# Strassen's scheme on pairs of feed-forward units, and the output projection in three blocks

## The chip, the cores and the metric

The kernel runs on one core of one Trainium2 chip. Its time is device microseconds from launch to end, the median of the runs. TensorE (PE) multiplies, VectorE (DVE), ScalarE (ACT) and GpSimd (POOL) do the elementwise work, and SyncE (SP) issues most of the DMAs.

## The reference

Two layers of an encoder trunk on 512 tokens of width 1024, in float32. Each layer has a feed-forward part, a token mixer with three branches, cross-attention into 256 memory tokens, and a second feed-forward part. The change touches the feed-forward parts alone:

```python
def rms_norm(x, g):
    xf = x.astype(jnp.float32)
    y = xf * lax.rsqrt(jnp.mean(xf * xf, axis=-1, keepdims=True) + EPS)
    return (y * g.astype(jnp.float32)).astype(x.dtype)

def swiglu(h, w_in, w_out):
    a, b = jnp.split(h @ w_in, 2, axis=-1)
    return (jax.nn.silu(a) * b) @ w_out
...
    for l in range(DEPTH):
        x = x + 0.5 * swiglu(rms_norm(x, ffn1_norm[l]), ffn1_w_in[l], ffn1_w_out[l])
...
        x = x + 0.5 * swiglu(rms_norm(x, ffn2_norm[l]), ffn2_w_in[l], ffn2_w_out[l])
```

`D_FF` is 2816, so `w_in` is 1024 x 5632 (a half for `a`, a half for `b`) and `w_out` is 2816 x 1024.

## The kernel before

Activations are held transposed: width on the 128 partitions (`KD` = 8 tiles, index k or m), the 512 tokens along the free dimension. Every matrix product keeps float32 accuracy by splitting both operands into a high part (type fp32r) and a low part, the rest. `mm3` issues three matmuls for a product: high x high, high x low, low x high.

Weights come from HBM as a stream in an order that `plan` fixes. `Stream.load` issues a DMA of a chunk (at most 128 x 2048) on SP's queue into one of `NSTAGE` = 2 staging tiles. `Stream.split` makes the high part on ACT (`whi`, L346) and the low part on DVE (`wlo`, L347) for up to 1024 columns, a "part"; there are `NW` = 4 buffers for each. `Stream.take` hands a part to the caller and first splits up to `LOOK` = 3 parts ahead.

A feed-forward call goes over 22 units of 128 columns of each half of `w_in` in 2 blocks of 11. In a unit, `pair_unit` fills two PSUM banks (psa, psb) with 2 x 8 x 3 matmuls of 512 columns, on x times the gain without the norm's row factor (`xh`, `xl`). The factor `s_row` is applied on the way out: DVE multiplies psa by it (L552), ACT takes the Silu (L553), POOL multiplies by it again (L554), DVE multiplies by psb (L555), and `split_to` makes the high and low parts (ACT L494, DVE L495). After a block, for each of 8 m, a bank takes 11 x 3 matmuls of the output projection and DVE adds half of it to x (L582). After the last block of a call, `nxt.tile(m)` writes the next norm's `xh`, `xl` (L428, L429) and sums squares (ACT L437, POOL L438). In the last call of the program the last m is done in two halves of 256 tokens, so that the final norm can begin with the first half.

Side tasks (generators in `tasks`) are advanced by `tick`. `mem_stats` is one: it loads the memory tokens and a table of constants and computes the norm of the memory. It is queued at the start of the program. `lam_prep` and others are held back with `issue_after`; otherwise a scheduler orders each engine's queue, and that order isn't always the order of the program. The engines run their queues in order. Buffers of the arena (`get`, `getr`) are quarters, halves or wholes of 14 tiles of 128 x 2048.

The mixer's rotary embedding runs on POOL (L747, L752, L754) beside DVE's work. The projection of the cross-attention keys (`xk`) uses `pair_unit` on the 256 memory tokens, so its matmuls have 256 columns.

Of the kernel before, what the change touches and what calls it, by code (L numbers as in the profile page):

```python
# [14 lines left out]
P = 128  # L15
# [10 lines left out]
NB = 2  # L26
JB = NJ // NB
# [46 lines left out]
def plan():  # L74
# [12 lines left out]

    def ffn(l, w_in, w_out):
        for b in range(NB):
            for j in range(b * JB, (b + 1) * JB):  # L90
                first = l == 0 and j == 0 and w_in == "ffn1_w_in"
                add((w_in, l, j), [256, 256, 512, 1024] if first else [1024, 1024], block(w_in, l, 0, KD, (j * P, D_FF + j * P), P))
            for m in range(KD):
                add((w_out, l, b, m), [768, 640], block(w_out, l, b * JB, JB, (m * P,), P))

# [168 lines left out]
def emit(tc, wts, par, rows, ws_t, bd, xt, memt, const, out):  # L264
# [40 lines left out]
    class Stream:  # L305
        def __init__(self):
            self.parts = []
            off = 0
            self.off = []
            for i, (key, cols, _) in enumerate(chunks):  # L310
                self.off.append(off)
                c0 = 0
                for n in cols:
                    self.parts.append((i, c0, n))
                    c0 += n
                off += c0 * P
# [4 lines left out]
            self.pos = 0  # L321

        def load(self, parts=None, between=None, eng=sp):
# [4 lines left out]
            t = stage_p.tile([P, 2048], F32, tag="stage", name="stage")  # L328
# [9 lines left out]

        def split(self):
            i, c0, n = self.parts[self.n_split]  # L340
            while i and self.n_load <= i + NSTAGE - 1 and self.n_load < len(chunks):
                self.load()
            t = self.loaded[i][:, c0:c0 + n]
# [6 lines left out]
            if c0 + n == sum(chunks[i][1]):  # L350
                del self.loaded[i]

        def take(self, key):
            i, c0, n = self.parts[self.pos]
            assert chunks[i][0] == key, (chunks[i][0], key)
# [178 lines left out]
    def ffn(l, w_in, w_out, norm, nxt):  # L534
        row, held = [], []
# [3 lines left out]

        for b in range(NB):  # L540
            gs = []
            for j in range(b * JB, (b + 1) * JB):
                held.append(pair_unit(w_in, l, j, xhk, xlk, hook=finish if norm is first and j == 1 else None))
                if norm is first and j == 0:
                    continue
                if not row:
                    finish()
                s_row = row[0]
                for psa, psb in held:
                    t = get(1)  # L550
                    g = getr(2)
                    dve.tensor_tensor(t.f, psa, s_row, op=ALU.mult)  # L552
                    mark["silu"] = act.activation(t.f, t.f, AF.Silu).ins  # L553
                    pool.tensor_tensor(t.f, t.f, s_row, op=ALU.mult)  # L554
                    dve.tensor_tensor(t.f, t.f, psb, op=ALU.mult)  # L555
                    mark["lo"] = split_to(g.r[:, 0:512], g.r[:, 512:1024], t.f)
                    t.free()
                    gs.append(g)
                    tick()
                held = []  # L560
            for m in range(KD):
                if b == NB - 1 and m == KD - 1 and isinstance(nxt, FinalNorm):
                    parts = [ws.take((w_out, l, b, m)) for _ in range(2)]
                    for h in range(2):
                        cs = slice(h * 256, h * 256 + 256)
                        ps = bank()[:, 0:256]
                        for k in range(JB):
                            hi, lo = parts[k // 6]
                            c = slice(k % 6 * P, (k % 6 + 1) * P)
                            mm3(ps, hi[:, c], lo[:, c], gs[k].r[:, 0:512][:, cs], gs[k].r[:, 512:1024][:, cs],  # L570
                                k == 0, k == JB - 1)
                        dve.scalar_tensor_tensor(x[:, m, cs], ps, 0.5, x[:, m, cs], op0=ALU.mult, op1=ALU.add)
                        nxt.half(h)
                    continue
                ps = bank()
                for h, (k0, k1) in enumerate(((0, 6), (6, 11))):
                    hi, lo = ws.take((w_out, l, b, m))
                    for k in range(k0, k1):
                        c = slice((k - k0) * P, (k - k0 + 1) * P)
                        mm3(ps, hi[:, c], lo[:, c], gs[k].r[:, 0:512], gs[k].r[:, 512:1024],  # L580
                            k == 0, k == JB - 1)
                dve.scalar_tensor_tensor(x[:, m], ps, 0.5, x[:, m], op0=ALU.mult, op1=ALU.add)  # L582
                if b == NB - 1:
                    nxt.tile(m)
                tick()
            for g in gs:
                g.free()
# [751 lines left out]
    tasks.append(mem_stats())  # L1339
# [30 lines left out]
```

## Time and profile before

| | before |
|---|---|
| median of 3 runs | 2640.4 us (2640.38 to 2642.13) |
| the profiled execution | 2639.9 us |
| its span in the profile | 2638.1 us |
| mean granted clock of TensorE | 0.998 of full |
| PE, DVE, ACT, POOL busy | 99%, 52%, 44%, 15% |
| matmuls in the trace | 12213 |
| HBM read | 250.27 MB, 96 GB/s over the span |

The profile describes one execution; its span runs from the first to the last instruction, and the time holds 1.8 us around it. Busy shares are averages over the whole span. Matmuls are pipelined: the duration that a row gives is longer than the distance to the next start, so rates are read from starts.

### The profile page before, as it was taken

What the parts mean: (1) busy time and instruction counts of PE and PEld (TensorE: products, weight loads), DVE (VectorE), ACT (ScalarE), POOL (GpSimd) and SP (SyncE); (2) the same over time, 40 slices, a digit from 0 to 9 for tenths busy, and PEclk for the clock granted to TensorE, in tenths of its full rate; (3) what the DMA queues carried; (4) which work ended last, traced back from release to release, by engine and by line L of the source; (5) the groups of instructions that cost most, each with busy time, mean ns of one, the idle gap of its engine ahead of it and who ended that gap; (6) DMA issues with size and microseconds to landing.
All of it is one profiled execution on the core that took longest, in us unless ns stands there. A gap on an engine that the chain in (4) does not pass through costs nothing.

```text
span 2638.1 us, 30190 instructions
## 1 busy us (share of the span) xinstructions
PE 2619.2 (99%) x12213; PEld 2183.8 (83%) x12213; DVE 1373.7 (52%) x1972; ACT 1164.3 (44%) x1659; POOL 390.5 (15%) x294
## 2 busy tenths in 40 slices
PE   9999999999999999999999999999999999999998
PEld 7888888788888888888888888887888888888886
DVE  5434457766656554334443344577675655543443
ACT  5322337967635442222332223479575444432223
POOL 1101115100021021011111011151000300210111
PEclk9999999999999999999999999999999999999999
DMA  5232232122233222232222322321222231322222
GB/s 182 81 133 96 82 108 83 67 90 72 96 108 116 88 104 91 93 112 81 103 96 87 127 96 78 119 87 56 88 80 104 96 128 64 112 86 99 111 76 76
DMA packets 49979, 254.31 MB, mean 96 GB/s; under 512 B 5168, under 2 KB 10928, under 8 KB 31664
## 3 DMA queue, kind: packets, MB, share of 16 engines
q1 hardware_dynamic: 49120, 250.30, 26.8%
q10 hardware_dynamic: 720, 2.09, 0.2%
q8 instruction: 95, 1.56, 0.2%
q14 instruction: 44, 0.36, 0.0%
HBM read 250.27 MB, written 2.10 MB: 96 GB/s over the span
## 4 chain that ended last, share of the span: by engine, by line
PE 95%; ACT 3%; DVE 1%; DMA 0%; issue 0%; DVEq 0%; ACTq 0%; POOL 0%; POOLq 0%
PE ps L367 30%; PE ps L365 30%; PE ps L366 30%; PE ps L891 1%; PE ps L879 1%; PE ps L862 1%; ACT whi L346 0%; DMA x<-in_xt 0%; PE ps L1192 0%; DVE slot L495 0%; ACT L668 0%; ACT L678 0%; ACT slot L1002 0%; PE ps L403 0%; DVE slot L481 0%
## 5 line engine op out<-in xcount | busy, mean ns | idle before, releaser
L346 ACT CAST whi<-stage 128x1024 fp32r<-128x1024 f32 (+2 forms) x506 | 491.4, 973 | 1002.5 <-PE ps L366 873.8
L347 DVE TENSOR_TENSOR wlo<-stage,whi 128x1024 fp32r<-128x1024 f32 (+2 forms) x506 | 587.3, 1162 | 471.9 <-ACT whi L346 470.0
L365 PE MATMUL ps<-xh,whi 128*128 128x512 f32 x2048 | 801.4, 391 | 5.0 <-DVE slot L1015 3.3
L366 PE MATMUL ps<-xl,whi 128*128 128x512 f32 x2048 | 798.0, 390 | 0.3 <-DVE xl L429 0.3
L367 PE MATMUL ps<-xh,wlo 128*128 128x512 f32 x2048 | 797.8, 390 | 0.0
L365 PE MATMUL ps<-slot,whi 128*128 128x512 f32 (+1 forms) x1291 | 487.5, 378 | 0.0
L366 PE MATMUL ps<-slot,whi 128*128 128x512 f32 (+1 forms) x1291 | 486.5, 377 | 0.0
L367 PE MATMUL ps<-slot,wlo 128*128 128x512 f32 (+1 forms) x1291 | 486.4, 377 | 0.0
L365 PEld LDWEIGHTS ps<-xh,whi 128*128 128x128 f32 x2048 | 384.8, 188 | 86.6 <-DVE slot L1015 4.9
L366 PEld LDWEIGHTS ps<-xl,whi 128*128 128x128 f32 x2048 | 385.0, 188 | 80.1 <-DVE xl L429 0.9
L367 PEld LDWEIGHTS ps<-xh,wlo 128*128 128x128 f32 x2048 | 384.8, 188 | 80.0
L554 POOL TENSOR_TENSOR slot<-slot,srow 128x512 f32<-128x512 f32 x88 | 148.2, 1685 | 921.2 <-ACT slot L553 921.2
L366 PEld LDWEIGHTS ps<-slot,whi 128*128 128x128 f32 x1291 | 243.0, 188 | 45.0 <-issue 0.5
L365 PEld LDWEIGHTS ps<-slot,whi 128*128 128x128 f32 x1291 | 242.9, 188 | 44.8 <-issue 0.5
L367 PEld LDWEIGHTS ps<-slot,wlo 128*128 128x128 f32 x1291 | 242.9, 188 | 44.6
L494 ACT CAST slot<-slot 128x512 fp32r<-128x512 f32 (+2 forms) x149 | 89.4, 608 | 296.6 <-DVE slot L555 216.3
L552 DVE TENSOR_TENSOR slot<-ps,srow 128x512 f32<-128x512 f32 x88 | 60.7, 691 | 214.1 <-PE ps L367 214.0
L438 POOL TENSOR_TENSOR nacc<-nacc,slot 128x512 f32<-128x512 f32 x55 | 84.4, 1535 | 550.0 <-ACT slot L437 284.1
L495 DVE TENSOR_TENSOR slot<-slot,slot 128x512 fp32r<-128x512 f32 (+2 forms) x149 | 105.5, 717 | 90.5 <-ACT slot L494 90.4
L555 DVE TENSOR_TENSOR slot<-slot,ps 128x512 f32<-128x512 f32 x88 | 60.5, 688 | 107.4 <-POOL slot L554 107.4
L495 DVE TENSOR_TENSOR slot<-ps,slot 128x512 fp32r<-128x512 f32 (+1 forms) x144 | 92.8, 655 | 39.5 <-ACT slot L494 38.7
L494 ACT CAST slot<-ps 128x512 fp32r<-128x512 f32 (+1 forms) x144 | 77.3, 562 | 56.4 <-PE ps L367 54.2
(194 smaller groups left out, 2252.2 us busy)
## 6 DMA issues: line engine op xcount, KB each, us to landing
stage<-in_wts SPq DMA_DIRECT2D x140, 1024.0 KB, 4.8
stage<-in_wts SPq DMA_DIRECT2D x64, 704.0 KB, 4.0
stage<-in_wts SPq DMA_DIRECT2D x77, 512.0 KB, 3.2
stage<-in_wts SPq DMA_DIRECT2D x8, 768.0 KB, 4.3
slot<-in_memt SPq DMA_DIRECT2D x6, 512.0 KB, 3.7
slot<-in_bd SPq DMA_DIRECT2D x4, 512.0 KB, 6.0
out<-slot SPq DMA_DIRECT2D x8, 256.0 KB, 2.5
x<-in_xt SPq DMA_DIRECT2D x1, 1024.0 KB, 8.4
```

Source lines behind the costliest of these rows:

```text
L346: mark["whi"] = act.copy(hi[:, 0:n], t).ins
L347: dve.tensor_tensor(lo[:, 0:n], t, hi[:, 0:n].bitcast(F32), op=ALU.subtract)
L365: pe.matmul(ps, lhsT=ah, rhs=bh, start=start, stop=False)
L366: pe.matmul(ps, lhsT=ah, rhs=bl, start=False, stop=False)
L367: pe.matmul(ps, lhsT=al, rhs=bh, start=False, stop=stop)
L438: self.adder.tensor_tensor(self.acc, self.acc, sq.f, op=ALU.add)
L494: act.copy(hi, src)
L495: return dve.tensor_tensor(lo, src, hi.bitcast(F32), op=ALU.subtract).ins
L552: dve.tensor_tensor(t.f, psa, s_row, op=ALU.mult)
L554: pool.tensor_tensor(t.f, t.f, s_row, op=ALU.mult)
L555: dve.tensor_tensor(t.f, t.f, psb, op=ALU.mult)
L862: pe.matmul(ps, lhsT=qt[e].r[:, c0:c0 + P], rhs=kk.r[:, k0:k0 + 512], start=part == 0, stop=part == 1)
```

## The change

Of the 22 units of a call, 4 stay as they were. The other 18 are done as 9 pairs. For a pair the weights of two units are seen as a 2 x 2 matrix of quarters (units by halves of k), for `a` and for `b`, and the activations as 2 x 2 quarters (halves of k by halves of the tokens). A scheme in Strassen's (Winograd's) form computes the same four output quarters from 7 products of sums of quarters instead of 8. In the code one product has both units of output side by side in one PSUM bank: 2 x 4 x 3 matmuls of 256 columns. The sums on the weights' side (S1 to S4) are made by POOL in `Stream.source` from the staged chunks P and Q, before the split; those on the activations' side by `combos` and `in_place`, once for a call, on x times gain times row factor. Seven products are combined by DVE on their way out of PSUM (`add`).

The blocks are `FB` = ((4, 2), (0, 4), (0, 3)): 4 units and 2 pairs, then 4 pairs, then 3 pairs, so the output projection runs in 3 blocks of 8, 8 and 6 k-steps. Its weight parts are one of 1024 or 768 columns for each m instead of two of 768 and 640. Pairs alternate between the staging tiles and two arena tiles (`slots`). `mem_stats` is queued before the last block's output projection in the first call.

```diff
-NB = 2
-JB = NJ // NB
+FB = ((4, 2), (0, 4), (0, 3))
...
+            for i in range(npair):
+                a, g = (j * P, j * P + P), (D_FF + j * P, D_FF + j * P + P)
+                side = (npair - i) % 2
+                add((w_in, l, "P", j, side), [2048], blocks(w_in, l, [(0, c) for c in a + g]))
+                add((w_in, l, "Q", j, side), [2048], blocks(w_in, l, [(4, c) for c in g + a]))
+                j += 2
             for m in range(KD):
-                add((w_out, l, b, m), [768, 640], block(w_out, l, b * JB, JB, (m * P,), P))
+                add((w_out, l, b, m), [(j - j0) * P], block(w_out, l, j0, j - j0, (m * P,), P))
...
+        PAIR = ("A11", "S1", "S2", "A12", "S3", "S4", "A22")
...
+        def room(self, i):
+            n = sum(self.side(j) == self.side(i) for j in self.loaded)
+            return n < (2 if self.side(i) and self.slots else 0 if self.side(i) else NSTAGE)
...
+        def source(self, i, nm):
+
+            a11, a21 = self.loaded[i][:, 0:1024], self.loaded[i][:, 1024:2048]
+            a22, a12 = self.loaded[i + 1][:, 0:1024], self.loaded[i + 1][:, 1024:2048]
+            if nm == "A11":
+                self.sums = [get(2), get(2)]
+                s1, s2 = (r.f for r in self.sums)
+                pool.tensor_tensor(s1, a21, a22, op=ALU.add)
+                pool.tensor_tensor(s2, s1, a11, op=ALU.add)
+                pool.tensor_tensor(a21, a21, a11, op=ALU.add)
+            s1, s2 = (r.f for r in self.sums)
+            if nm == "S4":
+                pool.tensor_tensor(s2, s2, a12, op=ALU.add)
+            return {"A11": a11, "S1": s1, "S2": s2, "A12": a12, "S3": a21, "S4": s2, "A22": a22}[nm]
...
-            while i and self.n_load <= i + NSTAGE - 1 and self.n_load < len(chunks):
+            while i and self.n_load <= i + pair + 3 and self.n_load < len(chunks) and self.room(self.n_load):
                 self.load()
...
+        def combos():
+            xn.extend([get(4), get(4)])
+            for m in range(KD):
+                dve.scalar_tensor_tensor(xn[m // 4].f[:, m % 4 * 512:(m % 4 + 1) * 512], x[:, m],
+                                         norm.gain[:, m:m + 1], row[0], op0=ALU.mult, op1=ALU.mult)
+            yield
+            b11, b12, b21, b22 = (quarter_of(h, t) for h in range(2) for t in range(2))
+            f = {}
+            for nm, a, b, op in (("S1", b11, b12, ALU.subtract), ("S2", b22, "S1", ALU.add),
+                                 ("S3", b12, b22, ALU.subtract), ("A22", b21, "S2", ALU.subtract)):
+                r = get(2)
+                c = r.f.rearrange("p (k c) -> p k c", k=4)
+                pool.tensor_tensor(c, a, f[b][1] if isinstance(b, str) else b, op=op)
+                f[nm] = r, c
+            for nm in ("S1", "S2", "S3", "A22"):
+                o = getr(4)
+                split_to(o.r[:, 0:1024], o.r[:, 1024:2048], f[nm][0].f)
...
+        def in_place():
+            for nm, h, t in (("A11", 0, 0), ("A12", 1, 0), ("S4", 1, 1)):
+                hi, lo = (a[:, 4 * h:4 * h + 4, t * 256:(t + 1) * 256] for a in (xh, xl))
+                split_to(hi, lo, quarter_of(h, t))
...
+            def product(nm):
+                ps = bank()
+                hi, lo = ws.take((w_in, l, "P", j), nm)
+                mh, ml, _ = mv[nm]
+                for i in range(2):
+                    for k in range(4):
+                        c = slice(i * 512 + k * P, i * 512 + (k + 1) * P)
+                        mm3(ps[:, i * 256:(i + 1) * 256], hi[:, c], lo[:, c], mh[k], ml[k],
+                            i == 0 and k == 0, i == 1 and k == 3)
+                return ps
...
+            act.copy(q1.f, product("A11"))
+            p5 = product("S1")
+            add(two(u2.f), product("S2"), q1, ALU.subtract)
+            add(two(w.f), p5, u2, ALU.subtract)
+            add(a4[:, :, 0], product("A12"), q1)
+            act.activation(a4[:, :, 0], a4[:, :, 0], AF.Silu)
+            p7 = product("S3")
+            add(two(u3.f), p7, u2)
+            add(b4[:, :, 1], p7, w, ALU.subtract)
+            add(a4[:, :, 1], product("S4"), w)
+            mark["silu"] = act.activation(a4[:, :, 1], a4[:, :, 1], AF.Silu).ins
+            add(b4[:, :, 0], product("A22"), u3)
...
+            dve.tensor_tensor(av.f, av.f, bv.f, op=ALU.mult)
+            g = getr(4)
+            mark["lo"] = split_to(g.r[:, 0:1024], g.r[:, 1024:2048], av.f)
...
+        for b, (nc, npair) in enumerate(FB):
+            for _ in range(nc):
                 held.append(pair_unit(w_in, l, j, xhk, xlk, hook=finish if norm is first and j == 1 else None))
...
+                if ws.slots is None:
+                    ws.slots = [get(4), get(4)]
+                    tasks.append(combos())
+                for ps in held:
+                    gated(*ps)
                     tick()
                 held = []
+            if nc:
+                drain()
+                in_place()
+            for _ in range(npair):
+                pair(j)
+                j += 2
+                tick()
...
+                if norm is first:
+                    tasks.append(mem_stats())
...
+                tail = last and m == KD - 1 and isinstance(nxt, FinalNorm)
+                for h in range(2 if tail else 1):
+                    cs = slice(h * 256, h * 256 + 256) if tail else slice(0, 512)
+                    ps = bank()[:, 0:cs.stop - cs.start]
+                    for k in range(nj):
+                        c = slice(k * P, (k + 1) * P)
+                        mm3(ps, hi[:, c], lo[:, c], gs[k][0][:, cs], gs[k][1][:, cs], k == 0, k == nj - 1)
+                    dve.scalar_tensor_tensor(x[:, m, cs], ps, 0.5, x[:, m, cs], op0=ALU.mult, op1=ALU.add)
...
-    tasks.append(mem_stats())
```

`gated` holds the six instructions that followed a unit before, unchanged.

## Rows read from the trace of the kernel before

**Rows 1.** The page, part 1: busy us, share of the span, instructions of each engine.

```profile
PE 2619.2 (99%) x12213; PEld 2183.8 (83%) x12213; DVE 1373.7 (52%) x1972; ACT 1164.3 (44%) x1659; POOL 390.5 (15%) x294
```

**Rows 2.** The page, part 4: the chain that ended last, shares by engine and line.

```profile
PE 95%; ACT 3%; DVE 1%; DMA 0%; issue 0%; DVEq 0%; ACTq 0%; POOL 0%; POOLq 0%
...
PE ps L367 30%; PE ps L365 30%; PE ps L366 30%; PE ps L891 1%; PE ps L879 1%; PE ps L862 1%; ACT whi L346 0%; DMA x<-in_xt 0%; PE ps L1192 0%; DVE slot L495 0%; ACT L668 0%; ACT L678 0%; ACT slot L1002 0%; PE ps L403 0%; DVE slot L481 0%
```

**Rows 3.** PE's waits: engine, line, releaser: us in total, times, longest.

```profile
PE ps L365 <- DVE slot L1015: 3.3, 2, 1.6
```

**Rows 4.** Timeline of PE in a feed-forward unit: start us, duration us, line, form.

```profile
99.71 0.39 PE L365 MATMUL ps<-xh,whi 128*128 128x512 f32 x1
...
105.15 0.39 PE L365 MATMUL ps<-xh,whi 128*128 128x512 f32 x1
```

**Rows 5.** Timeline of PE in the cross-attention key projection.

```profile
796.59 0.28 PE L365 MATMUL ps<-slot,whi 128*128 128x256 f32 x1
...
800.55 0.28 PE L365 MATMUL ps<-slot,whi 128*128 128x256 f32 x1
```

**Rows 6.** Timeline of DVE, ACT and POOL behind one feed-forward unit; idle before, releaser.

```profile
63.88 0.69 DVE L552 TENSOR_TENSOR slot<-ps,srow 128x512 f32<-128x512 f32 x1 [2.67 <-PE ps L367]
65.46 1.22 DVE L347 TENSOR_TENSOR wlo<-stage,whi 128x1024 fp32r<-128x1024 f32 x1 [0.90 <-ACT whi L346]
...
67.87 0.69 DVE L555 TENSOR_TENSOR slot<-slot,ps 128x512 f32<-128x512 f32 x1 [1.18 <-POOL slot L554]
69.25 0.69 DVE L495 TENSOR_TENSOR slot<-slot,slot 128x512 fp32r<-128x512 f32 x1 [0.69 <-ACT slot L494]
...
64.38 1.05 ACT L346 CAST whi<-stage 128x1024 fp32r<-128x1024 f32 x1 [4.44 <-PE ps L366]
65.33 0.63 ACT L553 ACTIVATE slot<-slot 128x512 f32<-128x512 f32 x1
68.59 0.62 ACT L494 CAST slot<-slot 128x512 fp32r<-128x512 f32 x1 [2.63 <-DVE slot L555]
...
66.04 1.79 POOL L554 TENSOR_TENSOR slot<-slot,srow 128x512 f32<-128x512 f32 x1 [9.14 <-ACT slot L553]
```

**Rows 7.** Timeline of DVE and POOL during the rotary embedding of the mixer.

```profile
437.46 2.29 DVE L495 TENSOR_TENSOR slot<-slot,slot 128x1024 fp32r<-128x1024 f32 x1 [3.38 <-ACT slot L494]
...
441.09 0.69 DVE L814 TENSOR_TENSOR slot<-ps,slot 64x512 fp32r<-64x512 f32 x1
...
442.53 2.22 DVE L347 TENSOR_TENSOR wlo<-stage,whi 128x1024 fp32r<-128x1024 f32 x1
...
437.38 1.28 POOL L747 TENSOR_TENSOR slot<-slot,slot 128x512 f32<-128x512 f32 x1
...
441.13 1.29 POOL L754 TENSOR_TENSOR slot<-slot,slot 128x512 f32<-128x512 f32 x1
442.38 1.29 POOL L747 TENSOR_TENSOR slot<-slot,slot 128x512 f32<-128x512 f32 x1
```

**Rows 8.** DVE's groups in the first feed-forward call; two POOL lines, ns min/median/max.

```profile
L347 DVE TENSOR_TENSOR wlo<-stage,whi 128x1024 fp32r<-128x1024 f32 x38 | 46.5, 1225 | 41.3 <-ACT whi L346 41.3
...
L552 DVE TENSOR_TENSOR slot<-ps,srow 128x512 f32<-128x512 f32 x22 | 15.1, 691 | 50.2 <-PE ps L367 50.2
...
L665 POOL TENSOR_TENSOR slot<-slot x5: 1288/1290/1294, 407.8 to 1807.0; 128x512 f32<-128x512 f32 x5
...
L606 POOL TENSOR_TENSOR slot<-cst,slot x8: 732/736/1290, 191.3 to 1500.8; 128x256 f32<-128x256 f32 x8
```

**Rows 9.** ACT's groups, forms apart: busy us, mean ns, idle before.

```profile
L346 ACT CAST whi<-stage 128x1024 fp32r<-128x1024 f32 x359 | 376.2, 1050 | 663.2 <-PE ps L366 579.3 <-issue 61.4 <-DMA stage<-in_wts 11.5
```

**Rows 10.** DMA issues: KB of each, median us from issue to landing.

```profile
stage<-in_wts SPq DMA_DIRECT2D x140, 1024.0 KB, 4.8
```

**Rows 11.** The chain at the end (start, us); windows: busy us by engine, clock, DMA.

```profile
2616.06 0.70 DVE x L582
...
2621.51 0.59 PE ps L405 x2
...
core 0: us, PE busy (x) PEld busy (x) DVE busy (x) ACT busy (x) POOL busy (x), PEclk, DMA share, GB/s
...
2616.00:2638.00 22.00, 10.45 (x75) 9.19 (x73) 10.55 (x16) 5.82 (x11) 4.79 (x3) 0.76 0.27 95
```

More of the change, by code (lines that the diff above doesn't have):

```diff
@@ L311, in __init__ @@
                 self.off.append(off)
[L312 to L316, printed above, removed]
+                off += sum(cols) * P
+                if key[2:3] == ("P",):
+                    self.parts += [(i, nm, 1024) for nm in self.PAIR]
+                elif key[2:3] != ("Q",):
+                    c0 = 0
+                    for n in cols:
+                        self.parts.append((i, c0, n))
+                        c0 += n
             self.loaded = {}
@@ L349, in split, with take @@
             self.n_split += 1
-            if c0 + n == sum(chunks[i][1]):
+            if pair and c0 == self.PAIR[-1]:
+                del self.loaded[i], self.loaded[i + 1]
+                for r in self.sums:
+                    r.free()
+            elif not pair and c0 + n == sum(chunks[i][1]):
                 del self.loaded[i]
-        def take(self, key):
+        def take(self, key, nm=None):
             i, c0, n = self.parts[self.pos]
-            assert chunks[i][0] == key, (chunks[i][0], key)
+            assert chunks[i][0][:len(key)] == key and nm in (None, c0), (chunks[i][0], key)
             while self.n_split < len(self.parts) and self.n_split <= self.pos + LOOK:
@@ L534, in ffn, with gated @@
     def ffn(l, w_in, w_out, norm, nxt):
-        row, held = [], []
+        row, held, gs = [], [], []
+        mv = {}
         def finish():
             row.append(norm.finish())
-        for b in range(NB):
-            gs = []
-            for j in range(b * JB, (b + 1) * JB):
+        def gated(psa, psb):
+            t = get(1)
+            g = getr(2)
+            dve.tensor_tensor(t.f, psa, row[0], op=ALU.mult)
+            mark["silu"] = act.activation(t.f, t.f, AF.Silu).ins
+            pool.tensor_tensor(t.f, t.f, row[0], op=ALU.mult)
+            dve.tensor_tensor(t.f, t.f, psb, op=ALU.mult)
+            mark["lo"] = split_to(g.r[:, 0:512], g.r[:, 512:1024], t.f)
+            t.free()
+            gs.append((g.r[:, 0:512], g.r[:, 512:1024], g))
@@ L543, in ffn @@
+        j = 0
+        for b, (nc, npair) in enumerate(FB):
+            for _ in range(nc):
                 held.append(pair_unit(w_in, l, j, xhk, xlk, hook=finish if norm is first and j == 1 else None))
-                if norm is first and j == 0:
+                j += 1
+                if norm is first and j == 1:
                     continue
@@ L586, in ffn @@
-            for g in gs:
-                g.free()
+            if nc:
[5 more added lines that the diff above has]
+                tick()
+            last = b == len(FB) - 1
+            if last:
+                for _, _, r in mv.values():
+                    if r is not None:
+                        r.free()
+                for r in ws.slots:
+                    r.free()
+                ws.slots = None
+                if norm is first:
+                    tasks.append(mem_stats())
@@ new lines, in ffn @@
+            nj = len(gs)
+            for m in range(KD):
+                hi, lo = ws.take((w_out, l, b, m))
+                tail = last and m == KD - 1 and isinstance(nxt, FinalNorm)
[6 more added lines that the diff above has]
+                    dve.scalar_tensor_tensor(x[:, m, cs], ps, 0.5, x[:, m, cs], op0=ALU.mult, op1=ALU.add)
+                    if tail:
+                        nxt.half(h)
+                if last and not tail:
+                    nxt.tile(m)
+                tick(2 if norm is first else 1)
@@ L590, in mixer @@
+            for _, _, g in gs:
+                if g is not None:
+                    g.free()
+            gs.clear()
     def mixer(l, norm, nxt):
```

81 lines of the change are left out of this document (44 added, 37 removed).

## Prediction

> **What bounds the kernel now.** I read the page's busy shares first: PE is busy for 2619.2 of 2638.1 us while DVE has 52%, ACT 44% and POOL 15% [rows 1]. A busy PE says little by itself, so next the chain of waits: 95% of it is PE, and the three lines of `mm3` have 30% each [rows 2]. Then PE's own waits: the longest kind sums to 3.3 us in the whole span [rows 3]. So the time is the number of matmuls times the distance between their starts, and that distance has to be read from starts: the 390 ns that a matmul "lasts" overlap with its neighbours. In a feed-forward unit the 25th of a row of 512-column matmuls starts 5.44 us after the 1st, 226.7 ns apart [rows 4]. The cross-attention keys are projected with 256-column matmuls, each with its own weight load, as the new products are; there 33 steps take 3.96 us, 120.0 ns apart [rows 5]. Half the columns cost 53% of the time. This ratio is what the change has to live on.
>
> **What it removes from PE.** Two plain units are 96 matmuls of 512 columns (8 k, 2 halves, 2 units, 3 matmuls each): 96 x 226.7 ns = 21.76 us. A pair is 7 products x 2 x 4 x 3 = 168 matmuls of 256 columns: 168 x 120.0 = 20.16 us. Instead of the eighth that the arithmetic promises, 1.60 us (7.4%) is left for a pair. There are 9 pairs in each of 4 feed-forward calls: 36 x 1.60 = **57.7 us less PE work**. The output projection keeps its 22 k-steps for every m, only split 8, 8, 6 in place of 11, 11; the 8 more evictions and adds for a call are DVE work of 0.69 us each, hidden by the 4 to 5 us of matmuls of an m.
>
> The Trainium skill ("TensorE: Matmul & The Clock Gate", section Back-to-back issue gap) gives 518 cycles at 2.4 GHz for 512 columns and 262 for 256; by it a pair would save 96 x 215.8 - 168 x 109.2 ns = 2.37 us, and all pairs 85 us. The trace does not agree with it (226.7 and 120.0 ns), and the sum goes by the rows.
>
> **What it adds beside PE.** For a pair, in 20.16 us:
> - ACT: 7 casts of weights at 1.05 us [rows 6, 9], one copy out of PSUM, two Silus at 0.63 us, one cast at about 1.05: some 10.3 us. Half busy, not a bound.
> - DVE: 7 subtractions for the weights' low parts at 1.22 us (4 before), a product and a low part of 1024 columns at about the same, and 7 combinations out of PSUM at 0.69 us [rows 6, 8]: 11.0 + 4.8 = 15.8 us.
> - POOL: 4 sums of 128x1024. No such shape is in the trace: 256 columns take 0.74 and 512 take 1.29 us [rows 8], 0.55 for 256 more, so I take 1.29 + 2 x 0.55 = 2.4 us each, 9.6 us for a pair.
>
> Each of the three fits into 20.16 us alone. But DVE and POOL do not run freely side by side. Where both read two SBUF tiles, one stands still: POOL starts at 437.38 and ends at 438.66; the DVE subtraction issued at 437.46 takes 2.29 us instead of 1.22 and ends 1.09 us after POOL has; at 442.38 the same, with 1.08. In between, DVE work that takes one input from PSUM lasts its 0.69 us right under a POOL instruction [rows 7]. The other way round POOL takes 1.79 instead of 1.29 us when it starts under a running subtraction [rows 6]. The Trainium skill calls this an exclusive lock on the pair of ports that the two engines share ("SBUF — State Buffer", section SBUF: two separate sides), held for the whole instruction, when DVE has two SBUF inputs; rows 7 agree.
>
> So count what takes turns: 9 DVE instructions with two SBUF inputs at 1.08 us and 4 POOL sums at 2.4: 19.3 us of 20.16. The 7 PSUM combinations (4.8 us) fit under POOL only where they happen to be next. Bounds for a pair: if every one is hidden PE stays the bound (20.16); if none is, 15.8 + 9.6 = 25.4 us. My value: POOL's sums come in a burst and alternate with subtractions, 4 x (2.4 + 1.08) = 13.9; the other 5 two-input instructions 5.4; between two of them stand 7/9 PSUM combinations, so about 3 of 7 are hidden and 2.7 us are not: **22.0 us**, 1.8 more than PE.
>
> This deficit need not reach PE. Weights are split three products ahead (`LOOK`), 3 x 2.88 = 8.6 us, of which cast and subtraction need 2.3: 6.3 us of slack. And only a pair that is followed by another in its block pays for the next one's three sums: 1, 3 and 2 of the 2, 4 and 3 pairs. The longest run collects 3 x 1.8 = 5.4 us, under 6.3. The last pair of a block has one POOL sum and recovers some 3.7 us of that (2.4 + 1.08 + 8 x 1.08 + 4.3 = 16.4 us of work). I take 3 us per call for what remains at a block's end and for a queue order that is not ideal: **12 us** in all (0 below, 102 above: at 25.4 us a pair, deficits of 5.2 give 9.4 + 4.2 us of stalls and 4.3 + 4.3 + 3.2 us of late block ends per call).
>
> **Ends of blocks.** Before, the last unit's chain (scale, Silu, POOL, product, cast, low part) ran from 63.88 to 69.94, 6.06 us [rows 6], and its result was needed only after 10 x 3 matmuls, 6.8 us: no wait. Now the last pair's chain is one combination 0.69, product 1.22, cast 1.05, low part 1.22, five handovers of 0.04 (as DVE 67.87 behind POOL in rows 6) and the last matmul's own tail (0.28 - 0.12): 4.5 us. With 8 units the result is used after 18 matmuls and one more, 4.3 us; with 6 after 12 and one, 2.9. Waits 0.3 + 0.3 + 1.6 = 2.2 us, **9 us** for four calls (0 if PE is given the next m's first steps ahead of the wait).
>
> **In front of the first pair.** `in_place` overwrites quarters of xh and xl that the fourth plain unit reads. Product A11 needs the quarter of k 0 to 3, free half way through that unit (5.4 us earlier), and its cast and subtraction take 2.3 us. In program order they stand behind the fourth unit's gating; but queues here aren't in program order: at 64.38 the cast of later weights runs ahead of the Silu of the finished unit [rows 6]. I take 1 us a call, **4 us**, for DVE being late after `combos` (8 scalings, 4 splits and 4 POOL sums in some 28 us, hidden by the plain units, whose parts last 5.4 us each); up to 27 if the order is that of the program (rival 2).
>
> **The rest.** The DMAs move the same bytes in 1 MB pieces of 4.8 us [rows 10], and a pair's two pieces have a pair's time to land: nothing, and if they came late, POOL's sums would be late first, then S1's weights. `mem_stats` moves from the start to the last block of the first call, past that call's weight loads on SP's queue; its 1.3 MB, 8 squares and POOL sums lie under 8 m of 4.1 us: nothing, and a late weight load would cost PE a few us once. The end: the last m in halves has 36 matmuls after the sixth in place of 66 [rows 11]; 15 matmuls of 512 (3.4 us) move ahead of it, while the chain behind it is bound by the sum of squares (2616.06 to the ones-matmul at 2621.51) more than by those matmuls and gets shorter by 0.8 to 3.6 us: -0.2 to +2.6, I take **+1.5**.
>
> **Sum.** Against the profiled execution's own 2639.9 us (2638.1 of span, 1.8 around it; the median of the runs shown is 2640.4, 0.02% above): 2639.9 - 57.7 + 12 + 9 + 4 + 1.5 = **2609 us**, 1.2% faster. Its own range is 2590 to 2626. A measurement of this kernel tells 0.2%, 5.3 us, from no change.
>
> **Rivals.**
> 1. DVE and POOL become the bound (20%). For it: rows 7, the 19.3 us of exclusive work in 20.16, and in-order queues. Against: the slack of 6.3 us and the short blocks. From 23.5 us a pair on nothing is won: deficits of 3.3 give about 11 us a call, 44 in all, and 2639.9 - 57.7 + 44 + 14.5 = 2641. At 25.4 it is 2639.9 - 57.7 + 102 + 14.5 = 2699. This is the case that ends slower.
> 2. The first quarter is split in program order (10%). PE then waits from the unit's end (63.88 plus 3 matmuls in rows 6, 64.56) until its low part at 69.94 and one subtraction more: 6.6 us, 27 in place of 4: 2632. Such holes would also let the clock fall, as it does to a mean of 0.76 in the tail, where PE is busy for 10.45 of 22 us [rows 11].
> 3. All of it is hidden (12%): PE stays gapless, 2639.9 - 57.7 + 1.5 = 2584.
> 4. 256-column matmuls with a weight load each don't hold 120 ns over a whole pair (2%). At 129.5 ns (21.76 us over 168) the gain is gone; rows 5 speak against it.
>
> **Chances.** Forecast 56%, rivals 20, 10, 12 and 2%. Faster takes the forecast, the third, most of the second: 74%. Within 0.2% 7%, slower 19%: nearly all of rival 1 and the fourth. The range runs from the third case into the lower part of the first, 2584 to 2650; above it lies most of rival 1.
>
> **What the profile after would show.** 256-column starts 120 ns apart inside a product; PE's waits under 40 us, and at ends of blocks on a slot's low part (L495 before); weight subtractions and POOL sums with long maxima, POOL near 2.4 us and above, but few PE waits on `wlo`. If PE waits inside pairs for `wlo` or for a free bank, rival 1 is right; a hole of some 6 us ahead of each first pair shows rival 2. The prediction is wrong if POOL's sums cost much more than 2.4 us, or if the static order leaves DVE waiting while subtractions stand behind.

## Result: slower, and the profile after

The changed kernel takes **2713.5 us** (median of 4 runs, 2712.3 to 2716.0) against 2640.6 us for the one before on the same chip: a ratio of 1.028, 95% interval 1.026 to 1.029. The forecast was 2609 us, so the time is 104 us above it and outside the range (2584 to 2650).

The page after, part 1 (compare [rows 1]): busy us, share of the span, instructions.

```profile
PE 2592.8 (96%) x14790; PEld 2276.2 (84%) x14790; DVE 1850.2 (68%) x2248; ACT 1300.4 (48%) x1761; POOL 739.3 (27%) x382
```

PE no longer fills the span of 2713.4 us, and the mean granted clock is 0.978 where it was 0.998. PE's waits, where [rows 3] had nothing above 3.3 us:

```profile
PE ps L420 <- ACT xh L549: 48.7, 4, 16.7
PE ps L421 <- DVE xl L550: 15.0, 4, 6.7
PE ps L422 <- DVE wlo L398: 12.2, 9, 2.3
PE ps L421 <- DVE slot L550: 8.9, 5, 2.6
PE ps L420 <- ACT slot L549: 7.5, 5, 2.9
PE ps L420 <- ACT whi L397: 6.5, 1, 6.5
```

The largest kind comes four times, once per call: the first product waits for A11's high part. L550 on `slot` and L549 on `slot` are the last pair's result at a block's end. In the pairs behind the first one only `wlo` is waited for; the wait for `whi` comes once, in the first call's first pair.

**Losses, stage by stage.** Waits don't count what a low clock costs, so I worked from starts on PE's timeline: a stage's length less its matmuls at 226.7 or 120.0 ns. Three starts of the second call (first unit, first product, first output projection) and two around the three-pair block of the first:

```profile
982.96 0.39 PE L420 MATMUL ps<-xh,whi 128*128 128x512 f32 x1
...
1041.50 0.58 PE L420 MATMUL ps<-xh,whi 128*128 128x256 f32 x1 [13.64 <-ACT xh L549]
...
1087.50 0.40 PE L420 MATMUL ps<-slot,whi 128*128 128x512 f32 x1
...
300.81 0.28 PE L420 MATMUL ps<-xh,whi 128*128 128x256 f32 x1
...
361.28 0.40 PE L420 MATMUL ps<-slot,whi 128*128 128x512 f32 x1
```

PE has 104.54 us from 982.96 to 1087.50 for 192 matmuls of 512 and 336 of 256 columns, ideally 43.52 + 40.32 = 83.84 us: 20.7 are lost. The three-pair block has 504 matmuls in 60.47 us, 120.0 ns each: nothing lost, and the price that the gain was worked out from is right to the digit. All stages of the four calls, against the prediction's terms:

| term | predicted, us | from starts, us |
|---|---|---|
| ahead of and in the first two pairs | 4 | 24.9 (without the program's first unit), 20.7, 20.8, 20.8: **87** |
| ends of blocks | 9 | 1.7 first blocks, 25.6 four-pair blocks (7.4, 5.0, 5.5, 7.6), about 2 last: **30** |
| inside pairs, late blocks | 12 | 12.9, all in four-pair blocks (3.3, 3.9, 2.4, 3.3) |
| tail (last m to the end) | 1.5 | 0.9 |

87 + 30 + 12.9 + 0.9 us is 104 above the prediction's 26.5 for the same four. The execution in the trace took 2716.0 us, 107 above the forecast. Most of the rest is at the program's start, for which the prediction had no term: PE's first unit begins 0.6 us later than before (6.96 against 6.39) and loses 6.5 us where it lost 3.1, with a granted clock of 0.50 from 10 to 18 us, 1.00 before. No run takes this part further.

**The hole ahead of the first pair**, second call. Windows (us; busy of PE, PEld, DVE, ACT, POOL; granted clock; DMA):

```profile
1024.00:1028.00 4.00, 3.86 (x17) 2.84 (x16) 3.21 (x4) 1.69 (x2) 2.48 (x1) 1.00 0.57 236
1028.00:1032.00 4.00, 0.00 (x0) 0.00 (x0) 0.00 (x0) 0.00 (x0) 3.92 (x3) 1.00 0.00 0
1032.00:1036.00 4.00, 0.00 (x0) 0.00 (x0) 0.00 (x0) 0.07 (x1) 4.00 (x3) 0.53 0.00 0
1036.00:1040.00 4.00, 0.00 (x0) 0.00 (x0) 2.85 (x2) 2.13 (x3) 4.00 (x3) 0.50 0.00 0
1040.00:1044.00 4.00, 0.58 (x1) 0.29 (x1) 4.00 (x3) 2.40 (x3) 2.71 (x1) 0.50 0.00 0
1044.00:1048.00 4.00, 2.41 (x11) 2.41 (x12) 4.00 (x4) 1.83 (x3) 3.52 (x2) 0.50 0.00 0
```

From 1028 to 1036 only POOL works; even DMA is idle. The timelines of POOL, ACT and DVE say why:

```profile
1025.52 3.36 POOL L380 TENSOR_TENSOR slot<-slot,slot 128x1024 f32<-128x1024 f32 x1 [4.86 <-issue]
1028.97 2.34 POOL L382 TENSOR_TENSOR slot<-slot 128x1024 f32<-128x1024 f32 x1
1031.26 2.34 POOL L381 TENSOR_TENSOR slot<-slot,slot 128x1024 f32<-128x1024 f32 x1
1033.56 2.34 POOL L380 TENSOR_TENSOR slot<-stage 128x1024 f32<-128x1024 f32 x1
1035.85 1.26 POOL L601 TENSOR_TENSOR slot<-slot,srow 128x512 f32<-128x512 f32 x1
1037.08 2.35 POOL L381 TENSOR_TENSOR slot<-slot,stage 128x1024 f32<-128x1024 f32 x1
...
1035.93 1.04 ACT L397 CAST whi<-slot 128x1024 fp32r<-128x1024 f32 x1 [8.00 <-POOL slot L380]
...
1039.46 1.04 ACT L397 CAST whi<-slot 128x1024 fp32r<-128x1024 f32 x1 [0.97 <-POOL slot L381]
1040.41 1.04 ACT L549 CAST xh<-slot 128x1024 fp32r<-128x1024 f32 x1
...
1037.15 0.69 DVE L602 TENSOR_TENSOR slot<-slot,ps 128x512 f32<-128x512 f32 x1 [9.89 <-POOL slot L601]
```

Read it from the end. A11's cast (ACT L549, 1040.41) stands behind two casts of weights' sums in ACT's queue, and those wait for POOL's sums. DVE waits 9.89 us for a gating product (L601) which POOL reaches only after four sums: those of both first pairs run back to back, as both have their weights loaded. The first three of the four are the second pair's (its quarters lie in `slot`, the first pair's in `stage`). The first pair's own first sum starts at 1033.56, though its weights had landed by 1027, when the DMA fell idle. In each call one to three of the second pair's sums stand ahead of the first pair's; no run changes this order alone. Between 1028.97 and 1035.85 the POOL sums take 2.34 us, the prediction's 2.4: nobody takes turns with them. They stand in one queue, and two other queues wait behind it.

**The end of the four-pair block**, first call; POOL, then DVE:

```profile
248.11 2.40 POOL L380 TENSOR_TENSOR slot<-slot,slot 128x1024 f32<-128x1024 f32 x1 [14.84 <-DMA slot<-in_wts]
250.58 3.26 POOL L381 TENSOR_TENSOR slot<-slot,slot 128x1024 f32<-128x1024 f32 x1
253.81 3.34 POOL L382 TENSOR_TENSOR slot<-slot 128x1024 f32<-128x1024 f32 x1
...
252.29 2.64 DVE L683 TENSOR_TENSOR slot<-slot 128x1024 f32<-128x1024 f32 x1
254.85 3.38 DVE L398 TENSOR_TENSOR wlo<-stage,whi 128x1024 fp32r<-128x1024 f32 x1
258.16 1.21 DVE L550 TENSOR_TENSOR slot<-slot,slot 128x1024 fp32r<-128x1024 f32 x1
```

Here they do take turns, as in [rows 7]. The weights of the next block's first pair have landed, so its three sums run while the last pair's chain does. The product (L683) takes 2.64 and a subtraction (L398) 3.38 us in place of about 1.2 each, so the last low part (L550) starts only at 258.16; afterwards the granted clock is 0.50 between 260 and 264 us.

### The profile page after: what moved, and what is told of

The parts are those of the page before. It is cut to its first block, busy times and chain, and to the rows that moved or that the text cites. A ratio compares the mean times of both kernels' runs of the same rounds, so it can differ in the third digit from the quotient of the medians.

```text
span 2713.4 us, 36079 instructions
## 1 busy us (share of the span) xinstructions
PE 2592.8 (96%) x14790; PEld 2276.2 (84%) x14790; DVE 1850.2 (68%) x2248; ACT 1300.4 (48%) x1761; POOL 739.3 (27%) x382
## 5 line engine op out<-in xcount | busy, mean ns | idle before, releaser
L420 PE MATMUL ps<-slot,whi 128*128 128x512 f32 (+1 forms) x2438 | 816.0, 335 | 14.0 <-ACT slot L549 7.5
L422 PE MATMUL ps<-slot,wlo 128*128 128x512 f32 (+1 forms) x2438 | 816.9, 335 | 11.4 <-DVE wlo L398 11.4
L421 PE MATMUL ps<-slot,whi 128*128 128x512 f32 (+1 forms) x2438 | 817.6, 336 | 8.9 <-DVE slot L550 8.9
L420 PE MATMUL ps<-xh,whi 128*128 128x512 f32 (+1 forms) x1760 | 602.9, 343 | 54.7 <-ACT xh L549 48.7
L398 DVE TENSOR_TENSOR wlo<-stage,whi 128x1024 fp32r<-128x1024 f32 (+2 forms) x394 | 526.6, 1338 | 179.7 <-ACT whi L397 176.8
L421 PE MATMUL ps<-xl,whi 128*128 128x512 f32 (+1 forms) x1760 | 600.0, 341 | 15.0 <-DVE xl L550 15.0
L422 PE MATMUL ps<-xh,wlo 128*128 128x512 f32 (+1 forms) x1760 | 599.0, 340 | 0.8 <-DVE wlo L398 0.8
L420 PEld LDWEIGHTS ps<-slot,whi 128*128 128x128 f32 x2438 | 465.6, 191 | 62.7 <-ACT slot L549 11.2
L422 PEld LDWEIGHTS ps<-slot,wlo 128*128 128x128 f32 x2438 | 466.7, 191 | 58.3 <-DVE wlo L398 12.9
L421 PEld LDWEIGHTS ps<-slot,whi 128*128 128x128 f32 x2438 | 467.0, 192 | 57.3 <-DVE slot L550 12.1
L397 ACT CAST whi<-slot 128x1024 fp32r<-128x1024 f32 x188 | 195.6, 1048 | 296.8 <-PE ps L421 212.5
L398 DVE TENSOR_TENSOR wlo<-slot,whi 128x1024 fp32r<-128x1024 f32 x188 | 254.5, 1358 | 38.1 <-ACT whi L397 37.8
L549 ACT CAST slot<-slot 128x512 fp32r<-128x512 f32 (+2 forms) x129 | 99.2, 779 | 251.5 <-DVE slot L683 87.0
L667 DVE TENSOR_TENSOR slot<-ps,slot 128x512 f32<-128x512 f32 x252 | 170.1, 687 | 55.1 <-PE ps L422 53.3
L550 DVE TENSOR_TENSOR slot<-slot,slot 128x512 fp32r<-128x512 f32 (+2 forms) x129 | 177.3, 1388 | 44.4 <-ACT slot L549 44.1
```

Source lines behind the costliest of these rows:

```text
L420: pe.matmul(ps, lhsT=ah, rhs=bh, start=start, stop=False)
L421: pe.matmul(ps, lhsT=ah, rhs=bl, start=False, stop=False)
L422: pe.matmul(ps, lhsT=al, rhs=bh, start=False, stop=stop)
L549: act.copy(hi, src)
L550: return dve.tensor_tensor(lo, src, hi.bitcast(F32), op=ALU.subtract).ins
L667: dve.tensor_tensor(out, two(ps), two(other.f), op=op)
```

## Experiments

Ratios are against the kernel before on the same chip. `dve` or `pool` in a diff is the engine that runs the line. The losses of each are in the table behind them.

**e1, plain units in a block of their own.**

```diff
-FB = ((4, 2), (0, 4), (0, 3))
+FB = ((4, 0), (0, 3), (0, 3), (0, 3))
```

> The four plain units become a block of their own with its output projection (8 m of 12 matmuls, some 21.8 us of PE work), and the 9 pairs follow in three blocks of 3. Backlog theory (the loss is PE waiting ahead of the first pair, while POOL works off the activations' sums, the weights' sums of two pairs and the gating, and the half clock in its wake): the four holes of some 16 us and most of the 31 us of slow clock go, one more block end per call costs 2 to 4 us; 2620 to 2640. Turns theory (DVE and POOL taking turns slow down every pair): nothing much moves, 2690 to 2715.

2683.8 us (1.0167, 1.0150 to 1.0184), a little under the slower of the two expectations and far above the other. Neither range was met. Next to nothing is lost ahead of the pairs (0.5 to 1.2 us in the last three calls), but the first block's end loses 8.1 to 11.4 us, the first three-pair block 1.4 to 4.3, and each end that pairs follow 3.3 to 6.6, two of them a call. The first block's end, second call; a window, then PE:

```profile
1020.00:1024.00 4.00, 2.13 (x9) 1.41 (x8) 2.77 (x4) 2.63 (x5) 0.91 (x1) 1.00 0.25 69
...
1025.78 0.80 PE L420 MATMUL ps<-slot,whi 128*128 128x512 f32 x1 [3.64 <-ACT slot L549]
```

POOL has little to do there (0.91 of 4 us) and makes no sum between 1008 and 1028. PE waits for the last plain unit's result, which is needed after only three k-steps. So POOL's weight sums aren't what is late at this end. At the later ends they are beside the chain again (the product L683 takes 3.40 us at 1114.08). A block of plain units by itself removes the hole, but at the price of these ends.

**e2, activations' sums on DVE.**

```diff
-                pool.tensor_tensor(c, a, f[b][1] if isinstance(b, str) else b, op=op)
+                dve.tensor_tensor(c, a, f[b][1] if isinstance(b, str) else b, op=op)
```

> The four sums on the activations' side, once per call, move from POOL to DVE; the pairs are untouched. Backlog theory: POOL has four sums of 2.8 us less of about eleven ahead of the first pair, DVE four of 1.2 us more; each hole shrinks by 7 to 11 us and its slow clock by some 2 us: 2660 to 2685. Turns theory: the pairs cost what they did, within 5 us of 2713.

2690.8 us in one run. The loss ahead of the first pairs falls from 20.8 to 14.0 a call, less than was expected; the ends stay.

**e3, POOL's weight sums left out** (the products S1 to S4 take a quarter in place of the sum).

```diff
-                pool.tensor_tensor(s1, a21, a22, op=ALU.add)
-                pool.tensor_tensor(s2, s1, a11, op=ALU.add)
-                pool.tensor_tensor(a21, a21, a11, op=ALU.add)
...
-                pool.tensor_tensor(s2, s2, a12, op=ALU.add)
```

> POOL's four sums on the weights' side are left out in all pairs, the products take plain quarters in their place (so part of the computation is left out); splits, matmuls and everything else stay. Both theories win here, at different places. Backlog theory: 2595 to 2620, the hole ahead of the first pair shrinks to under 6 us, which is what the place of A11's cast in the queue costs by itself. Turns theory: 2570 to 2590, and the holes stay while the pairs get faster.

2631.0 us in one run: 82 us less, so these sums are most of the loss, and the four-pair blocks and their ends are clean. But 9.4 a call stay ahead of the first pairs, with PE waiting 21.6 us in four waits for A11's high part; the expectation missed that by 11 us and more.

**e4, three blocks of plain units** (no pairs, so no sums).

```diff
-FB = ((4, 2), (0, 4), (0, 3))
+FB = ((8, 0), (8, 0), (6, 0))
...
-                    tasks.append(combos())
...
-                in_place()
...
```

> All 22 units plain, in three blocks of 8, 8 and 6, no pairs and no sums: the new output projection, the moved memory statistics and the shorter tail alone. Both theories: 2640 within 4 us. If it is slower by more than 8 us, part of the loss belongs to the blocks and not to the pairs.

2654.3 us (1.0052, 1.0037 to 1.0067), 10 us above what was expected. In the second call the three output projections lose 0.8, 0.8 and 1.2 us, 11 in four calls; before, the same count is 0.0 (264 matmuls of 512 in 59.84 us). A third block is not free: after 8 or 6 k-steps the last unit's 6.06 us chain [rows 6] is late. The rest of the 14 us above the kernel before is mostly at the program's start (4.7 us lost in the first unit, 3.1 before) and in the tail.

**e5, all weight sums on DVE.**

```diff
-                pool.tensor_tensor(s1, a21, a22, op=ALU.add)
+                dve.tensor_tensor(s1, a21, a22, op=ALU.add)
...
-                pool.tensor_tensor(s2, s2, a12, op=ALU.add)
+                dve.tensor_tensor(s2, s2, a12, op=ALU.add)
```

> All four sums of a pair's weights are made by VectorE instead of GpSimd; GpSimd keeps the activations' sums and the gating products. Theory (turns: a GpSimd sum of 2.4 us holds VectorE's two-SBUF-input work off, and VectorE holds GpSimd off in turn, so that GpSimd's in-order queue is what is late): VectorE makes such a sum in about 1.1 to 1.2 us, a pair then has 13 instructions of that kind and 7 combinations of 0.69 us, 19 to 20.5 us of VectorE beside 20.16 us of TensorE, and there is nothing to take turns with. The loss ahead of the first pairs (20.7 to 24.3 us a call) falls to about 10, the loss at the end of the four-pair block (5.0 to 7.6) to about 2; VectorE close to full inside pairs gives back up to 3 us a call. 2713 - 45 - 17 + 8, so 2650 to 2670. Rival (what counts is the sum of elementwise work that has to be done ahead of the first products, on whichever engine): VectorE is late by as much as GpSimd was, 2700 to 2730.

2645.6 us (1.0022, 1.0013 to 1.0032): 68 us less than the changed kernel, a little better than the theory said. Four-pair blocks lose nothing, their ends 0.6, the first pairs 13.3. The amount of work is not the matter: DVE has 36 x 4 more instructions and is late nowhere else. What the run can't tell apart is a sum's price, the turns and the queue's order, which all change with the engine: in the second call one of the second pair's sums (1005.48) stands ahead of the first pair's (1006.61), where on POOL it was three.

**e6, A11 in a buffer of its own, split early.**

```diff
+            o = getr(4)
+            split_to(o.r[:, 0:1024].rearrange("p (k c) -> p k c", k=4), o.r[:, 1024:2048].rearrange("p (k c) -> p k c", k=4), quarter_of(0, 0))
...
             yield
...
-            for nm, h, t in (("A11", 0, 0), ("A12", 1, 0), ("S4", 1, 1)):
+            for nm, h, t in (("A12", 1, 0), ("S4", 1, 1)):
```

> The first quarter A11 of the activations gets a buffer of its own and is split with the first step of the sums, in place of being written over the quarter of xh and xl that the fourth plain unit still reads; all else as in the changed kernel. Theory (the second rival of the prediction has a share of its own: the cast of A11 stands in ScalarE's queue behind casts that wait for GpSimd's weight sums): the first product starts 5 to 9 us earlier a call, but the next products still wait for GpSimd's sums, so half of that is given back: 2685 to 2702. Rival (GpSimd's late sums set the end of the hole whatever comes first): 2707 to 2718. Rival (only A11's place matters): the hole is gone, about 2635 to 2650.

2705.4 us (1.0248, 1.0231 to 1.0265), between the theory's range and the rival's, nearer to the rival's. PE no longer waits for `xh` ahead of the pairs, but now 40.2 us for `wlo` and 11.7 for `whi`. Half of the 40.2 (19.9 us) comes while the plain units still run:

```profile
1026.60 0.79 PE L422 MATMUL ps<-xh,wlo 128*128 128x512 f32 x1 [7.52 <-DVE wlo L398]
```

That low part stands in DVE's queue behind a gating product (L602, 1023.19) which waits 3.46 us for POOL, and POOL made two of the second pair's sums first. Of the rest, 8.8 us are in the four-pair blocks; the others are products of the first pairs, which now wait for POOL's sums themselves. Alone, A11's place is worth 2 us a call.

**e7, e5 and e6 together, with the activations' sums on DVE too** (edits of e2, e5 and e6).

> Weights' and activations' sums all on VectorE, and A11 in a buffer of its own, split early; GpSimd keeps the gating alone. Theory of turns: both causes of the hole ahead of the first pairs are gone; what is left is 2 to 5 us a call there, 2 us at the end of the four-pair block and up to 3 us of a full VectorE: 2713 - 70 - 17 + 8, so 2625 to 2645. Rival (amount of elementwise work): VectorE has 13 + 4 + 8 more instructions to do beside the plain units and stays late: 2680 or more.

**2613.9 us (0.990, 0.989 to 0.992): faster than before**, and 11 us below the theory's range. Ahead of the first pairs 4.8 a call is left. The timeline of DVE there shows another limit:

```profile
57.42 1.22 DVE L380 TENSOR_TENSOR slot<-stage 128x1024 f32<-128x1024 f32 x1
58.55 1.22 DVE L550 TENSOR_TENSOR slot<-slot,slot 128x1024 fp32r<-128x1024 f32 x1
59.69 1.22 DVE L381 TENSOR_TENSOR slot<-slot,stage 128x1024 f32<-128x1024 f32 x1
60.82 1.22 DVE L382 TENSOR_TENSOR stage<-stage 128x1024 f32<-128x1024 f32 x1
```

A sum takes 1.22 us and the next starts 1.13 later, against 2.34 and more on POOL. But DVE's queue is now full while the plain units end, and the first products' low parts stand in it (PE waits 10.8 us for `wlo`).

**e8, the next block's first sum waits for the last pair** (a small POOL sum that reads the last low part stands ahead).

```diff
+                if chunks[i - 1][0][0].endswith("w_out"):
+                    pool.tensor_tensor(s1[:, 0:256], behind[0], behind[0], op=ALU.add)
                 pool.tensor_tensor(s1, a21, a22, op=ALU.add)
...
+            behind[:] = [g.r[:, 1024:1280].bitcast(F32)]
```

> The changed kernel, but GpSimd's first weight sum of a block waits for the last pair of the block before: a short GpSimd sum that reads that pair's low part stands ahead of it. Theory (the loss of 5.0 to 7.6 us at the end of the four-pair block is the last pair's chain stretched by the next block's first sums, with what the clock loses behind the hole): that loss falls to about 1.5 us, 17 us less in all: 2693 to 2702. Rival (the loss comes from weights of the output projection that land late, or from the chain's own length): 2711 to 2720.

2697.1 us in one run, where the theory had it; the four-pair block's end falls from 6.1 to 0.5 a call and the rest stays. POOL's first row (the small sum, released by the low part L553) and DVE's chain at the place shown above:

```profile
254.58 0.61 POOL L381 TENSOR_TENSOR slot<-slot 128x256 f32<-128x256 f32 x1 [22.85 <-DVE slot L553]
...
250.94 1.23 DVE L686 TENSOR_TENSOR slot<-slot 128x1024 f32<-128x1024 f32 x1
252.08 1.22 DVE L400 TENSOR_TENSOR wlo<-stage,whi 128x1024 fp32r<-128x1024 f32 x1
253.27 1.23 DVE L553 TENSOR_TENSOR slot<-slot,slot 128x1024 fp32r<-128x1024 f32 x1
```

The same three instructions (L683, L398 and L550 in the changed kernel) take 1.23, 1.22 and 1.23 us where they took 2.64, 3.38 and 1.21, and the clock stays at 1.00. The Trainium skill ("SBUF — State Buffer", section SBUF: two separate sides) describes this as a lock that the two engines share; these rows and those of [rows 7] agree.

**e9, weight sums on DVE and the early A11** (edits of e5 and e6).

> The weights' sums on VectorE and A11 in its own early buffer, but the activations' sums left on GpSimd: it stands between the kernel with all weights' sums on VectorE (2645.6 us) and the one that has both moves and the activations' sums on VectorE too (2613.9). Theory A (what is left of the hole once GpSimd's queue is short is A11's place: its cast stands behind casts that wait): the whole difference comes with A11, 2610 to 2622. Theory B (four sums of the activations on GpSimd, each taking turns with VectorE, are what is late): 2632 to 2645.

2636.0 us in one run. Of the 31.7 us between e5 and e7, 9.6 come with A11's place and 22 with the activations' sums leaving POOL: Theory B for the most part, and the time lies in its range.

**e10, six plain units and one pair in the first block** (on e7; 8 pairs a call).

```diff
-FB = ((4, 2), (0, 4), (0, 3))
+FB = ((6, 1), (0, 4), (0, 3))
```

> The version with all sums on VectorE and the early A11 (2613.9 us), with blocks of 6 plain units and 1 pair, 4 pairs, 3 pairs: 8 pairs a call in place of 9. It gives up 4 x 1.60 = 6.4 us of TensorE's gain. Theory (what is left there, 3 to 7 us a call ahead of the first pairs, is VectorE's load in the four plain units, which now spreads over six): that loss falls to about 1 a call, 2613.9 + 6.4 - 17 = 2600 to 2607. Rival (the loss is a chain that starts with the last plain unit, whatever lies ahead): 2618 to 2622.

**2604.8 us (0.987, 0.985 to 0.988), the fastest version**, in the theory's range. No pair loses anything, and no kind of PE's waits is above 3.3 us, as before the change [rows 3]; the two largest:

```profile
PE ps L420 <- DVE slot L1176: 3.3, 2, 1.6
PE ps L422 <- DVE wlo L398: 2.8, 2, 2.1
```

A pair less in each call costs 6.4 us of TensorE's gain, and yet the kernel is 9.1 us faster than e7. The edit does two things: it spreads DVE's load over six units, and it takes the second pair's sums out of the first block. e11 does only the second.

**e11, one pair in the first block, 9 pairs** (on e7).

```diff
-FB = ((4, 2), (0, 4), (0, 3))
+FB = ((4, 1), (0, 4), (0, 4))
```

> The same version with blocks of 4 plain units and 1 pair, 4 pairs, 4 pairs: still 9 pairs. Only one pair's weight sums fall into VectorE's busy stretch, and the output projection with little VectorE work follows. Theory (VectorE's load): a third to a half of the loss ahead of the pairs goes, 2600 to 2608, less some 1 us a call if the end of the first block with its 6 k-steps (result needed after 2.9 us, chain 4.5) waits: 2602 to 2612. Rival (chain behind the last plain unit): 2612 to 2620.

2609.4 us (0.988, 0.987 to 0.990), in the theory's range. In the last three calls the first block is clean with only four plain units, so leaving out the second pair is enough there; in the first call its pair still loses 7.3 us, where e10's loses nothing. The block's end with 6 k-steps loses 4.0, 3.0 and 5.8 us in those three, more than the 1 that the theory gave it.

**e12, no weight sums, and the early A11** (e3 with the edit of e6; the products again take quarters in place of sums).

> No sums of weights at all are made (the products take quarters in place of sums, so the output is not the reference's), and A11 is split early into its own buffer. Without the early A11 the same kernel took 2631.0 us and lost 8.5 to 10.2 us a call ahead of the first pairs. Theory A (this loss is A11's place in the queue, the second rival of the prediction, 6.6 us a call with the clock's share on top): the loss falls to 0 to 2, so 2591 to 2602. Theory B (the activations' sums on GpSimd and VectorE's own work are late): 2618 to 2631. In either case nothing but 7 products stands against 2584, the prediction's floor.

2609.5 us in one run, between the two theories: without the weights' sums A11's place is worth 6.3 us a call, and 3.1 stay. The distance to 2584 was not taken apart further.

Losses in us a call, means over calls two to four, worked out as above (0.5 of the first column is there before too):

| kernel | time | units and first pairs | four-pair block | end of first block | end of four-pair block |
|---|---|---|---|---|---|
| changed | 2713.5 | 20.8 | 3.2 | 0.5 | 6.1 |
| e2 | 2690.8 | 14.0 | 3.1 | 0.8 | 6.2 |
| e3 | 2631.0 | 9.4 | 0.0 | 0.5 | 0.5 |
| e5 | 2645.6 | 13.3 | 0.0 | 0.6 | 0.6 |
| e6 | 2705.4 | 18.8 | 2.9 | 0.5 | 5.8 |
| e7 | 2613.9 | 4.8 | 0.0 | 0.5 | 0.7 |
| e8 | 2697.1 | 21.6 | 3.9 | 0.5 | 0.5 |
| e9 | 2636.0 | 9.4 | 0.0 | 1.2 | 0.8 |
| e10 | 2604.8 | 0.5 | 0.0 | 1.0 | 0.4 |
| e11 | 2609.4 | 0.5 | 0.0 | 4.3 | 0.6 |
| e12 | 2609.5 | 3.1 | 0.0 | 0.4 | 0.5 |

## Why the prediction was wrong

**What held.** 1.60 us of TensorE time a pair: products ran at 120.0 ns wherever nothing was late. The 12 us for pairs that fall behind came out at 12.9, in part by luck: they were set for what is left at a block's end and for the queue's order, while the measured ones lie inside the four-pair blocks, where PE waits up to 2.3 us for a low part, and the three-pair blocks lose nothing. They come from POOL's sums: they are gone in e3 and in e5. A POOL sum alone takes 2.34 us (2.4 was taken), and the tail cost 0.9 (1.5). And e10 shows that the gain is there to be had.

**The step that failed: "In front of the first pair", 4 us taken, 87 measured.** It named 8 scalings, 4 splits and 4 POOL sums in 28 us and called them hidden by the plain units. It left out that seven weights' sums of the first two pairs join the same POOL queue at the same time, with the gating products among them and the second pair's partly ahead of the first's. The sums were counted per pair in the steady state, 9.6 of 20.16 us, where they indeed cost little; at the start of a call two pairs' sums have no pair to hide under. The prediction looked at each engine's share of a stage, and not at what stands ahead of what: PE waited for ACT, ACT for POOL, DVE for POOL. e5 with e3 shows the weights' sums as the larger part (7.5 to 11.4 of the 20.8), e2 and e9 against e7 the activations' (6.8 and 4.6), e6 and e3 against e12 A11's place (2.0 with the long queue, 6.3 without weight sums). They don't add up to a fixed split, since each hides the others; together they bring the hole down to 4.8 (e7), and it is gone only when the first block has one pair (e10, and e11 in the last three calls). How much of it is a sum's price on POOL and how much the order of the sums stays open; turns cost nothing from 1028.97 to 1035.85, where the sums took 2.34 us each.

**The second step: "Ends of blocks", 9 us taken, 30 measured.** The chain was priced at its undisturbed 4.5 us. The prediction had said that only a pair followed by another in its block pays for the next one's sums; the sums of the next block's first pair run as soon as their weights land, which is in this chain. e8 moves them and takes 5.6 a call away. (The 0.8 to 1.2 us that an end costs in e4 belong to blocks that end in a plain unit; the changed kernel has none.)

**The rivals.** The first rival had the right engines and ended on the right side, near the measured time with its 2699, but by luck: its at most 102 us were a deficit of every pair, some 54 inside pairs and 47 at block ends. Measured are 12.9 and 30, and the largest loss, ahead of the pairs, isn't in it. The second named A11's place and foresaw that such holes let the clock fall; both happened, with waits of 4.8 to 16.7 us, but in the changed kernel alone the place was worth 2 us a call (e6), not 6.6, because something else was late next.

## What to carry to other kernels

Price added elementwise work at the place where it is densest, the start of a stage and its seams, not as a share of the steady state; there write down each in-order queue, in the order in which the trace or the scheduler has it, and who waits for its last item. Here the sums that feed TensorE belonged on the engine that makes them fastest and without turns, although it is the busier one: moving them from POOL to DVE, with one quarter split earlier, turned 2.8% slower into 1.0% faster. Where a stage was too full, giving up a pair there (e10) was worth more than the pair.

## What the runs showed of the hardware

The clock made the holes dearer. In the second call PE stands still from 1027.9 to 1041.5; the granted clock is 1.00 until 1032, 0.53 over 1032 to 1036 and 0.50 (1.2 of 2.4 GHz) until 1048, when products are running again. In the first call, products at 0.50 start 213.0 ns apart in place of 120.0 (23 steps in 4.90 us):

```profile
81.33 0.41 PE L422 MATMUL ps<-xh,wlo 128*128 128x256 f32 x1
...
86.23 0.41 PE L422 MATMUL ps<-slot,wlo 128*128 128x256 f32 x1
```

DVE can be nearly full without cost: in e5's and e7's four-pair blocks it makes 13 instructions of 128x1024 (1.13 us apart at best) and 7 combinations per 20.16 us of TensorE, and no product starts late. POOL's 128x1024 sums average 2.60 to 3.34 us by group beside DVE, against 2.34 alone.
